# Two products in place of three per weight tile, for the 256-token stages of a two-layer diffusion backbone

## The chip, the cores and the metric

One core of a Trainium2 chip. The metric is the device time of one execution in microseconds, the median over runs. Compute engines of the core: TensorE (PE in the profile, with PEld for its weight loads), VectorE (DVE), ScalarE (ACT), GpSimd (POOL). SyncE (SP) issues the transfers. Matmuls write into PSUM, which the kernel uses as eight banks of 128 partitions x 512 fp32.

## The reference: what is computed

Two layers over 256 latent tokens with a prefix of 256 context tokens, width 1024. A layer is a half-step SwiGLU, a mixer and a second half-step SwiGLU, each behind an RMSNorm with shift, scale and gate:

```python
h = ffn_half_step(h, ...); hc = ffn_half_step(hc, ...)          # 1024 -> 2 x 2816 -> 1024
nq, nk, nv, fu, wq, wk, wv, gl = split_projection(u @ w_in[l])  # one combined projection
a = neighbourhood_attention(...); f = fourier_mix(fu); w = window_gqa_attention(...)
h = h + gt2 * merge_branches(a, f, w, gl, w_br[l], w_out[l])    # sigmoid gate per branch
if not last: (the same for the context tokens)
h = ffn_half_step(h, ...)
```

The context tokens are dropped after the mixer inputs of the last layer. So everything of layer 0, and of layer 1 up to the keys and values, runs over 512 tokens; the queries, gates, merge and second SwiGLU of layer 1 run over 256.

## The kernel before, in words

Activations lie transposed, 128 channels on the partitions and the tokens along the free dimension. To keep fp32 accuracy, each weight chunk and each activation is split into a high part (rounded to fp32r) and a low part (the rest). A product of a 128 x 128 weight tile with an activation is then three matmuls into one PSUM bank, `mm3` (lines 285 to 290): high weight with high activation (L288), high weight with low activation (L289), low weight with high activation (L290). For 512 tokens each of them has 512 columns, for 256 tokens 256.

Weights come in a fixed order as 424 chunks of eight tiles (`Weights`): a DMA on SP's queue, the high part on ACT (L66), the low part on DVE or POOL (L75, `lo_engine`), both some two chunks ahead of PE. `load_to`, `hi_to` and `lo_to` are called from `next`, so these instructions stand in the engines' queues where the weight stream crosses a chunk's start or middle. The program order is kept on each engine (`manual_schedule`); each engine works through its own queue in that order.

The stages of layer 1 that run over n = 256 tokens:

- `mix` (line 828 on; `attention` from line 694): `attention` goes step by step; a step issues, in this order, the normalising of older blocks (DVE L730 to L736), `small_part` (DVE L748), `transposes` (PE L741, ACT L743), `weights` of the block (DVE L717 takes the row maximum over the scores, then ACT L719 the exponentials), `values` (PE L759, ACT L765 at the end of a block), and then `fill`. `fill` first runs up to two pending pieces (`pieces`), then places projection matmuls among the steps. A pending piece is the taking out of a finished projection: `rope`, `plain`, or for gates `raw` (line 898 on: one ACT copy, L903, from PSUM to SBUF). Twelve of the 24 gate projections of layer 1 are placed in this way (`EARLY_GATES`); in attention the low weights are made on POOL.
- `merge` (line 1033 on): per output block j the remaining gate projections and their sigmoids (ACT L1052), three branch projections of four tiles, each multiplied with its gate on DVE (L1070), and the sum (L1073, L1074). The last block splits the seven earlier sums first (`split_s`), then its own. Then `project_out` with w_out.
- `ffn` (line 504 on) with n = 256: `first` makes four banks at once while the norm delivers its channels; then groups of 16 tiles, two banks each, taken out by `swish`: silu on ACT (L511), product on DVE (L512), high part on ACT (L297), low part on DVE (L298). Each half of 11 such groups is followed by `project_out` with w2, eight groups of 11 tiles, each taken out by `add_to_h` on DVE (L467).
- `stat` collects the squares for the next norm on POOL (last block: ACT L462), and the norm's chain (L173 to L191, L205 to L213) stands between `project_out` and the next stage; `finish` (L1084) writes the output.

Activations are tiles of 128 x 512 from one pool, `N_ACT` of them; the two parts of an activation are two tiles, also where only 256 of the 512 columns are used.

## Time and profile before

| | |
|---|---|
| median of 3 runs | 2100.93 us (2100.38 to 2104.16) |
| profiled execution, device time | 2101.61 us |
| its span in the trace | 2099.8 us |
| PE busy | 2049.5 us, 98% |
| DVE busy | 1282.1 us, 61% |
| ACT busy | 838.4 us, 40% |
| POOL busy | 340.6 us, 16% |

The 1.81 us between span and device time lie around the span. A busy PE is not PE at its peak: a matmul's record is longer than the step from one start to the next, so the steps have to be read from the order of time. Line numbers (L288) are those of the kernel before. In rows of the order of time the columns are the start, the time, the engine, the line and operation, the tiles, the count, and in brackets the idle time of the engine before it with what ended it.

### The profile page before, as it was taken

What the parts mean: (1) busy time and instruction counts of PE and PEld (TensorE: products, weight loads), DVE (VectorE), ACT (ScalarE), POOL (GpSimd) and SP (SyncE); (2) the same over time, 40 slices, a digit from 0 to 9 for tenths busy, and PEclk for the clock granted to TensorE, in tenths of its full rate; (3) what the DMA queues carried; (4) which work ended last, traced back from release to release, by engine and by line L of the source; (5) the groups of instructions that cost most, each with busy time, mean ns of one, the idle gap of its engine ahead of it and who ended that gap; (6) DMA issues with size and microseconds to landing.
All of it is one profiled execution on the core that took longest, in us unless ns stands there. A gap on an engine that the chain in (4) does not pass through costs nothing. (4 is left out here: it accounts for less than half of the span.)

```text
span 2099.8 us, 28967 instructions
## 1 busy us (share of the span) xinstructions
PE 2049.5 (98%) x11193; PEld 1764.6 (84%) x11193; DVE 1282.1 (61%) x2035; ACT 838.4 (40%) x1362; POOL 340.6 (16%) x238
## 2 busy tenths in 40 slices
PE   7999999999999999999999999999999989999998
PEld 2788888978888888988888898888888878999998
DVE  6777777465686335677777566533336568566554
ACT  4422222355787223432222243222224468645443
POOL 4200000402442111300000120000012155330002
PEclk8999999999999999999999999999999999999999
DMA  7455656445532333466666646623334463565653
GB/s 274 140 201 180 201 201 210 129 131 151 139 85 72 99 99 92 140 190 193 196 191 191 212 144 198 200 91 101 100 118 141 135 191 109 161 182 159 187 177 109
DMA packets 103010, 326.64 MB, mean 156 GB/s; under 512 B 13396, under 2 KB 18516, under 8 KB 102872
## 3 DMA queue, kind: packets, MB, share of 16 engines
q1 hardware_dynamic: 102872, 324.79, 49.6%
q8 instruction: 88, 1.44, 0.3%
q14 instruction: 50, 0.41, 0.1%
HBM read 305.60 MB, written 1.05 MB: 146 GB/s over the span
## 5 line engine op out<-in xcount | busy, mean ns | idle before, releaser
L289 PE MATMUL ps<-act,wh 128*128 128x512 f32 (+1 forms) x3227 | 1121.4, 348 | 10.6 <-DVE act L228 9.8
L288 PE MATMUL ps<-act,wh 128*128 128x512 f32 (+1 forms) x3227 | 1122.1, 348 | 2.1 <-ACT act L207 1.1
L290 PE MATMUL ps<-act,wl 128*128 128x512 f32 (+1 forms) x3227 | 1120.1, 347 | 1.8 <-DVE wl L75 1.8
L289 PEld LDWEIGHTS ps<-act,wh 128*128 128x128 f32 x3227 | 613.6, 190 | 86.7 <-DVE act L228 10.5
L290 PEld LDWEIGHTS ps<-act,wl 128*128 128x128 f32 x3227 | 613.7, 190 | 78.1 <-DVE wl L75 2.6
L288 PEld LDWEIGHTS ps<-act,wh 128*128 128x128 f32 x3227 | 613.6, 190 | 77.5 <-ACT act L207 1.4
L66 ACT ACTIVATE wh<-raw 128x1024 fp32r<-128x1024 f32 x424 | 436.4, 1050 | 318.4 <-PE ps L289 281.7
L75 DVE TENSOR_TENSOR wl<-raw,wh 128x1024 fp32r<-128x1024 f32 x379 | 473.3, 1261 | 102.6 <-ACT wh L66 102.6
L310 DVE CUSTOM_DVE_ANT_0 dump<-ada,silu_row 128x1024 bf16<-128x1024 f32 x224 | 273.4, 1221 | 12.2 <-DMA ada<-in_w_ada 9.9
L297 ACT ACTIVATE act<-tmp 128x512 fp32r<-128x512 f32 (+1 forms) x122 | 66.8, 566 | 431.5 <-DVE tmp L512 413.3
L450 POOL TENSOR_TENSOR tmp<-h 128x512 f32<-128x512 f32 (+1 forms) x7 | 11.4, 1634 | 1125.3 <-DVE h L467 797.6
L467 DVE SCALAR_TENSOR_TENSOR h<-ps,mod,h 128x256 f32<-128x256 f32 x136 | 61.7, 481 | 199.7 <-PE ps L290 199.7
L512 DVE TENSOR_TENSOR tmp<-tmp,ps 128x512 f32<-128x512 f32 (+1 forms) x88 | 54.6, 621 | 208.6 <-PE ps L290 203.1
L75 POOL TENSOR_TENSOR wl<-raw,wh 128x1024 fp32r<-128x1024 f32 x45 | 111.4, 2477 | 225.9 <-ACT wh L66 215.1
L298 DVE TENSOR_TENSOR act<-tmp,act 128x512 fp32r<-128x512 f32 (+1 forms) x122 | 74.3, 626 | 61.0 <-ACT act L297 61.0
L511 ACT ACTIVATE tmp<-ps 128x512 f32<-128x512 f32 (+1 forms) x88 | 47.8, 543 | 123.4 <-PE ps L290 122.8
L456 POOL TENSOR_TENSOR tmp<-h 128x256 f32<-128x256 f32 (+1 forms) x44 | 64.4, 1463 | 107.0 <-DVE h L467 104.4
L719 ACT ACTIVATE tmp<-tmp,sm 128x512 f32<-128x512 f32 (+1 forms) x96 | 62.1, 647 | 32.4 <-DVE sm L717 32.2
L748 DVE TENSOR_TENSOR act<-ps,act 128x512 fp32r<-128x512 f32 x80 | 54.9, 686 | 30.1 <-ACT act L743 27.5
L759 PE MATMUL ps<-act 128*128 128x256 f32 x320 | 62.5, 308 | 10.3 <-DVE act L748 9.2
L743 ACT ACTIVATE act<-ps 128x512 fp32r<-128x512 f32 x80 | 47.5, 594 | 46.2 <-PE ps L741 44.7
L1070 DVE TENSOR_TENSOR tmp<-tmp,ps 128x512 f32<-128x512 f32 (+1 forms) x48 | 26.0, 551 | 62.3 <-PE ps L290 61.0
(110 smaller groups left out, 1322.1 us busy)
## 6 DMA issues: line engine op xcount, KB each, us to landing
raw<-in_ws SPq DMA_DIRECT2D x424, 512.0 KB, 4.2
ada<-in_w_ada SPq DMA_DIRECT2D x128, 512.0 KB, 3.7
act<-act SPq DMA_DIRECT2D x112, 128.0 KB, 2.4
tmp<-in_w_ada_sc SPq DMA_DIRECT2D x16, 256.0 KB, 5.7
tmp<-in_w_ada SPq DMA_DIRECT2D x16, 256.0 KB, 6.0
masks<-in_na_bias SPq DMA_DIRECT2D x8, 512.0 KB, 5.0
h<-in_h SPq DMA_DIRECT2D x8, 256.0 KB, 5.5
act<-act SPq DMA_DIRECT2D x32, 64.0 KB, 3.4
```

The lines of the kernel that those rows point to most:

```text
L66: self.nc.scalar.activation(out=wh, in_=self.raw[i], func=AF.Copy)
L75: self.lo_engine.tensor_tensor(out=wl, in0=self.raw.pop(i), in1=self.hi[i].bitcast(F32), op=ALU.subtract)
L288: mm(ps, lhsT=w[0], rhs=x[0], start=start, stop=False)
L289: mm(ps, lhsT=w[0], rhs=x[1], start=False, stop=False)
L290: mm(ps, lhsT=w[1], rhs=x[0], start=False, stop=stop)
L297: nc.scalar.activation(out=hi, in_=src, func=AF.Copy)
L298: nc.vector.tensor_tensor(out=lo, in0=src, in1=hi.bitcast(F32), op=ALU.subtract)
L310: self.nc.vector.tensor_tensor_reduce(out=self.dump[:, ks], in0=w, in1=self.silu_row[:, v, ks], scale=1.0, scalar=m if half else 0.0, op0= ...
L456: nc.gpsimd.tensor_tensor(out=sq, in0=h, in1=h, op=ALU.mult)
L467: self.nc.vector.scalar_tensor_tensor(out=h, in0=ps, scalar=self.mod[l, g][:, v, j:j + 1], in1=h, op0=ALU.mult, op1=ALU.add)
L719: nc.scalar.activation(out=e[:, :nk], in_=e[:, :nk], func=AF.Exp, scale=-1.0, bias=nm, accum_out=b["sum"][:, i:i + 1])
L759: nc.tensor.matmul(b["ps"][hp][:, :256], lhsT=v, rhs=t[j][:, cs], start=c == 0 and j == 0, stop=c == n - 1 and j == 1)
```

## The change

For n = 256 the two parts of an activation now lie side by side in one 128 x 512 tile (`parts`, `pair`; the norm's output in a pool of its own, eight tiles [128, 2, 512], with `N_ACT` lowered from 60 to 44). `mm3` takes such a tile and makes two matmuls: the high weight with all 512 columns, which leaves high x high in the left half of the bank and high x low in the right half, and the low weight with the 256 high columns, added to the right half. Whoever takes the bank out adds the halves: `fold` copies the right half to SBUF on ACT and adds it to the left half, in PSUM, on DVE (in `swish` for both banks, in `merge` for each gate still to be made and each branch); `raw` has its ACT copy of the left half followed by a DVE addition of the right half; `project_out` calls `add_to_h` twice. It holds for the 12 early gates, for `merge`, w_out and the second SwiGLU of layer 1; with n = 512, and for the queries of layer 1, three products remain.

```diff
-N_ACT = 60
+N_ACT = 44
...
+        self.pair_p = pool("pair", KD)
...
+    def pair(self):
+        return self.pair_p.tile([128, 2, NT], F32R, tag="pair", name="pair")
+    def parts(self, n):
+        if n > NT // 2:
+            return self.act()[:, :n], self.act()[:, :n]
+        return self.act().rearrange("p (s t) -> p s t", s=2)
+    def fold(self, *pss):
+        n, t = NT // 2, self.tmp()
+        for i, ps in enumerate(pss):
+            self.nc.scalar.activation(out=t[:, i * n:i * n + n], in_=ps[:, n:], func=AF.Copy)
+        for i, ps in enumerate(pss):
+            self.nc.vector.tensor_tensor(out=ps[:, :n], in0=ps[:, :n], in1=t[:, i * n:i * n + n], op=ALU.add)
...
         mm = self.nc.tensor.matmul
+        if not isinstance(x, tuple):
+            half = lambda: mm(ps[:, NT // 2:], lhsT=w[1], rhs=x[:, 0, :], start=False, stop=False)
+            if stop:
+                half()
+            mm(ps, lhsT=w[0], rhs=x, start=start, stop=stop)
+            if not stop:
+                half()
+            return
...
+            if n < NT:
+                self.add_to_h(ps[:, :n], l, gate, j, 0)
+                self.add_to_h(ps[:, n:], l, gate, j, 0)
...
             s = self.tmp()
+            if n < NT:
+                self.fold(pa, pb)
             nc.scalar.activation(out=s[:, :n], in_=pa[:, :n], func=AF.Silu)
...
             nc.scalar.activation(out=t, in_=ps[:, :n], func=AF.Copy)
+            if n < NT:
+                nc.vector.tensor_tensor(out=t, in0=t, in1=ps[:, n:], op=ALU.add)
             res[name] = t
             yield
...
+                    if n < NT:
+                        self.fold(x)
                 nc.scalar.activation(out=t[:, :n], in_=x[:, :n], func=AF.Sigmoid)
...
-                    self.mm3(ps[:, :n], w, parts[b][k], k == 0, k == 3)
+                    self.mm3(ps, w, parts[b][k], k == 0, k == 3)
+                if n < NT:
+                    self.fold(ps)
                 nc.vector.tensor_tensor(out=sg[b][:, :n], in0=sg[b][:, :n], in1=ps[:, :n], op=ALU.mult)
```

## Rows read from the trace of the kernel before

**Rows 1.** The page, busy time of each engine over the span.

```profile
PE 2049.5 (98%) x11193; PEld 1764.6 (84%) x11193; DVE 1282.1 (61%) x2035; ACT 838.4 (40%) x1362; POOL 340.6 (16%) x238
```

**Rows 2.** Groups of instructions by line and shape, PE, whole span: one of the three products with 256 columns.

```profile
L288 PE MATMUL ps<-act,wh 128*128 128x256 f32 x1318 | 375.2, 285 | 2.1 <-ACT act L207 1.1 <-ACT act L297 0.8 <-ACT wh L66 0.2
```

**Rows 3.** Order of time on PE, a stretch of the second SwiGLU of layer 1 (256 columns): the first row and the 25th matmul after it.

```profile
1949.91 0.28 PE L290 MATMUL ps<-act,wl 128*128 128x256 f32 x1
...
1952.91 0.28 PE L288 MATMUL ps<-act,wh 128*128 128x256 f32 x1
```

**Rows 4.** The same for a stretch of layer 1 with 512 columns: the first row and the 8th matmul after it.

```profile
1349.62 0.39 PE L289 MATMUL ps<-act,wh 128*128 128x512 f32 x1
...
1351.43 0.39 PE L288 MATMUL ps<-act,wh 128*128 128x512 f32 x1
```

**Rows 5.** Busy time by stretch: us, PE, PEld, DVE, ACT, POOL (count each), granted clock of PE, DMA share, GB/s.

```profile
1700.00:1760.00 60.00, 50.52 (x379) 46.26 (x378) 44.23 (x92) 45.34 (x107) 34.14 (x27) 1.00 0.48 143
1760.00:1800.00 40.00, 39.71 (x316) 37.96 (x315) 24.92 (x53) 31.52 (x72) 19.33 (x10) 1.00 0.37 114
...
1900.00:2080.00 180.00, 180.00 (x1494) 180.00 (x1493) 102.27 (x129) 82.21 (x112) 10.40 (x8) 0.99 0.54 173
```

**Rows 6.** Busy time by stretch of 10 us, the same columns: two stretches in which PE stood idle.

```profile
1700.00:1710.00 10.00, 7.19 (x53) 6.24 (x52) 5.04 (x14) 6.03 (x13) 2.39 (x1) 1.00 0.61 246
...
1890.00:1900.00 10.00, 7.55 (x46) 6.67 (x45) 5.68 (x13) 4.67 (x8) 2.20 (x2) 0.78 0.29 95
```

**Rows 7.** The chain of work that ended last, pieces in order of time, within the attention of layer 1 (start, us, what).

```profile
1724.45 0.81 ACT tmp L719 x2
...
1749.89 0.27 ACT tmp L903
...
1774.53 0.62 PE ps L759 x3
```

**Rows 8.** Who waited for whom, same stretch (total us, times, longest): the second piece of `rope` on DVE behind its first on ACT.

```profile
DVE act L893 <- ACT act L891: 8.5, 5, 1.9
```

**Rows 9.** Order of time on ACT, attention of layer 1: gate copies (L903), and two of the exponentials (L719) behind the first and the third.

```profile
1726.75 0.39 ACT L903 ACTIVATE tmp<-ps 128x256 f32<-128x256 f32 x1
...
1727.51 0.72 ACT L719 ACTIVATE tmp<-tmp,sm 128x512 f32<-128x512 f32 x1
...
1736.43 0.37 ACT L903 ACTIVATE tmp<-ps 128x256 f32<-128x256 f32 x1
...
1749.79 0.36 ACT L903 ACTIVATE tmp<-ps 128x256 f32<-128x256 f32 x1
...
1750.54 0.72 ACT L719 ACTIVATE tmp<-tmp,sm 128x512 f32<-128x512 f32 x1
...
1766.40 0.38 ACT L903 ACTIVATE tmp<-ps 128x256 f32<-128x256 f32 x1
...
1771.00 0.36 ACT L903 ACTIVATE tmp<-ps 128x256 f32<-128x256 f32 x1
...
1778.38 0.39 ACT L903 ACTIVATE tmp<-ps 128x256 f32<-128x256 f32 x1
```

**Rows 10.** Order of time on DVE, same stretch: for each gate copy above the next long DVE instruction in program order, and for the first gate also the row maximum (L717) after it.

```profile
1724.41 0.67 DVE L748 TENSOR_TENSOR act<-ps,act 128x512 fp32r<-128x512 f32 x1
...
1726.06 0.69 DVE L717 CUSTOM_DVE_ANT_1 tmp<-ps,masks 128x512 f32<-128x512 f32 x1 [0.19 <-PE ps L708]
...
1735.68 0.69 DVE L748 TENSOR_TENSOR act<-ps,act 128x512 fp32r<-128x512 f32 x1 [0.30 <-ACT act L743]
...
1748.77 0.69 DVE L748 TENSOR_TENSOR act<-ps,act 128x512 fp32r<-128x512 f32 x1
1749.45 0.75 DVE L717 CUSTOM_DVE_ANT_1 tmp<-ps,masks,nsink 128x512 f32<-128x512 f32 x1
...
1764.06 0.69 DVE L748 TENSOR_TENSOR act<-ps,act 128x512 fp32r<-128x512 f32 x1 [1.01 <-ACT act L743]
...
1770.30 0.69 DVE L748 TENSOR_TENSOR act<-ps,act 128x512 fp32r<-128x512 f32 x1 [1.26 <-ACT act L743]
...
1776.04 0.69 DVE L748 TENSOR_TENSOR act<-ps,act 128x512 fp32r<-128x512 f32 x1 [0.82 <-ACT act L743]
```

**Rows 11.** Who waited for whom on PE (total us, times, longest), at the start of `merge` (1795 to 1812 us) and at its end (1860 to 1882 us).

```profile
PE ps L290 <- DVE wl L75: 0.8, 1, 0.8
```

```profile
PE ps L288 <- ACT act L297: 0.8, 1, 0.8
```

**Rows 12.** Order of time on DVE at the end of `merge`: two gate products in a row.

```profile
1867.92 0.74 DVE L1070 TENSOR_TENSOR tmp<-tmp,ps 128x256 f32<-128x256 f32 x2
```

**Rows 13.** Order of time on DVE, the taking out of one group of the second SwiGLU of layer 1, and on ACT the silu of the next.

```profile
1951.74 0.42 DVE L512 TENSOR_TENSOR tmp<-tmp,ps 128x256 f32<-128x256 f32 x1 [1.54 <-PE ps L290]
1952.64 0.42 DVE L298 TENSOR_TENSOR act<-tmp,act 128x256 fp32r<-128x256 f32 x1 [0.48 <-ACT act L297]
1953.59 2.36 DVE L75 TENSOR_TENSOR wl<-raw,wh 128x1024 fp32r<-128x1024 f32 x2 [0.53 <-ACT wh L66]
```

```profile
1954.55 0.38 ACT L511 ACTIVATE tmp<-ps 128x256 f32<-128x256 f32 x1
```

**Rows 14.** Order of time on DVE at the very end: the last `add_to_h`, and the eight multiplications of `finish`, of the same shape.

```profile
2089.91 0.48 DVE L467 SCALAR_TENSOR_TENSOR h<-ps,mod,h 128x256 f32<-128x256 f32 x1 [3.48 <-PE ps L290]
...
2093.16 3.22 DVE L1084 SCALAR_TENSOR_TENSOR tmp<-h,g_fin,ps 128x256 f32<-128x256 f32 x8 [1.04 <-PE ps L191]
```

More of the change, by code (lines that the diff above doesn't have):

```diff
@@ L202, in _step @@
             if v == 0:
-                self.u[k] = (em.act(), em.act())
+                self.u[k] = em.pair()
             hs = em.tmp()[:, :256]
@@ L206, in _step @@
                                            op0=ALU.mult, op1=ALU.mult)
-            nc.scalar.activation(out=self.u[k][0][:, s], in_=hs, func=AF.Identity, bias=sh[:, v, k:k + 1])
+            nc.scalar.activation(out=self.u[k][:, 0, s], in_=hs, func=AF.Identity, bias=sh[:, v, k:k + 1])
             self.work[t] = hs
@@ L211, in _step @@
             s = slice(v * 256, (v + 1) * 256)
-            hi, lo = self.u[k]
+            hi, lo = self.u[k][:, 0, :], self.u[k][:, 1, :]
             nc.vector.scalar_tensor_tensor(out=lo[:, s], in0=self.work.pop(t - 1), scalar=sh[:, v, k:k + 1],
@@ L221, in _first @@
         sh, sc = em.mod[self.l, 3 * self.g], em.mod[self.l, 3 * self.g + 1]
-        hi, lo = self.u[k] = em.act(), em.act()
+        self.u[k] = em.pair()
+        hi, lo = self.u[k][:, 0, :], self.u[k][:, 1, :]
         for out in (hi, u32):
@@ L277, in act, with two @@
         return self.act_p.tile([128, NT], F32R, tag="act", name="act")
+    def pair(self):
[4 more added lines that the diff above has]
+        return self.act().rearrange("p (s t) -> p s t", s=2)
+    def two(self, x):
+        return x if isinstance(x, tuple) else (x[:, 0, :], x[:, 1, :])
+    def fold(self, *pss):
[4 more added lines that the diff above has]
+            self.nc.vector.tensor_tensor(out=ps[:, :n], in0=ps[:, :n], in1=t[:, i * n:i * n + n], op=ALU.add)
     def tmp(self):
@@ L478, in group @@
                 w = self.W.next(tiles(j, k))
-                self.mm3(ps[:, :hi - lo], w, (x[k][0][:, lo:hi], x[k][1][:, lo:hi]), k == 0, k == kx - 1)
+                if n == NT:
+                    self.mm3(ps[:, :hi - lo], w, (x[k][0][:, lo:hi], x[k][1][:, lo:hi]), k == 0, k == kx - 1)
+                else:
+                    self.mm3(ps, w, x[k], k == 0, k == kx - 1)
+            if n < NT:
+                self.add_to_h(ps[:, :n], l, gate, j, 0)
+                self.add_to_h(ps[:, n:], l, gate, j, 0)
+                if nxt is not None:
+                    self.stat(j, 0, n)
+                return
             for v in range(lo // 256, hi // 256):
@@ L510, in swish @@
             s = self.tmp()
+            if n < NT:
+                self.fold(pa, pb)
             nc.scalar.activation(out=s[:, :n], in_=pa[:, :n], func=AF.Silu)
             nc.vector.tensor_tensor(out=s[:, :n], in0=s[:, :n], in1=pb[:, :n], op=ALU.mult)
-            gh, gl = self.act(), self.act()
-            self.split(s[:, :n], (gh[:, :n], gl[:, :n]))
-            return gh, gl
+            g = self.parts(n)
+            self.split(s[:, :n], self.two(g))
+            return g
         def first(passes):
@@ L534, in first @@
                             norm.stage2(1)
-                    x = tuple(t[:, lo:hi] for t in norm.u[k])
+                    x = norm.u[k][:, :, lo:hi]
+                    x = self.two(x) if n == NT else x
                     for q in range(4):
                         w = W.next((w13, l, k * 128, (q % 2) * DFF + (q // 2) * 128))
-                        self.mm3(pss[q][:, lo:hi], w, x, k == 0, k == KD - 1)
+                        self.mm3(pss[q][:, lo:hi] if n == NT else pss[q], w, x, k == 0, k == KD - 1)
             W.lo_engine = nc.vector
@@ L547, in ffn @@
                 u = norm.all()
-                ux = [(a[:, :n], b[:, :n]) for a, b in u]
+                ux = [self.two(a) if n == NT else a[:, :, :n] for a in u]
             self.W.on_tile = lambda: self.bg.step(1)
@@ L555, in ffn @@
                         w = W.next((w13, l, k * 128, ab * DFF + i * 128))
-                        self.mm3(pss[ab][:, :n], w, ux[k], k == 0, k == KD - 1)
+                        self.mm3(pss[ab], w, ux[k], k == 0, k == KD - 1)
                 g.append(swish(*pss))
@@ L581, in project_rows @@
                 s = slice(lo + t * 128, lo + (t + 1) * 128)
-                mm(ps, lhsT=u[k][0][:, s], rhs=w[0], start=k == 0, stop=False)
-                mm(ps, lhsT=u[k][0][:, s], rhs=w[1], start=False, stop=False)
-                mm(ps, lhsT=u[k][1][:, s], rhs=w[0], start=False, stop=k == KD - 1)
+                mm(ps, lhsT=u[k][:, 0, s], rhs=w[0], start=k == 0, stop=False)
+                mm(ps, lhsT=u[k][:, 0, s], rhs=w[1], start=False, stop=False)
+                mm(ps, lhsT=u[k][:, 1, s], rhs=w[0], start=False, stop=k == KD - 1)
         return pss
@@ L676, in along_channels @@
             ys[fc] = None
-            f = self.act()[:, :n], self.act()[:, :n]
+            f = self.parts(n)
             self.split(ps[:, :n].rearrange("p (s e k) -> p s e k", e=2, k=128),
-                       [a.rearrange("p (s k e) -> p s e k", e=2, k=128) for a in f])
+                       [a.rearrange("p (s k e) -> p s e k", e=2, k=128) for a in self.two(f)])
             out.append(f)
@@ L844, in project @@
             ps = self.ps()
+            side = name[0] == "gate" and n < NT
             for k in range(KD):
                 w = W.next(("w_in", l, k * 128, cols))
-                self.mm3(ps[:, :n], w, (u[k][0][:, :n], u[k][1][:, :n]), k == 0, k == KD - 1)
+                x = u[k][:, :, :n]
+                self.mm3(ps if side else ps[:, :n], w, x if side else self.two(x), k == 0, k == KD - 1)
                 if k == KD - 1:
@@ L984, in split_out @@
         def split_out(o, p):
-            hi, lo = self.act()[:, :n], self.act()[:, :n]
+            t = self.parts(n)
+            hi, lo = self.two(t)
             nc.scalar.activation(out=hi, in_=o[p][:, :n], func=AF.Copy)
@@ L989, in split_out @@
             nc.vector.tensor_tensor(out=lo, in0=o[p][:, :n], in1=hi.bitcast(F32), op=ALU.subtract)
-            o[p] = hi, lo
+            o[p] = t
         def left(o, p, lat):
@@ L1037, in split_s @@
         def split_s(x):
-            t = (self.act(), self.act())
-            self.split(x[:, :n], (t[0][:, :n], t[1][:, :n]))
-            return t[0][:, :n], t[1][:, :n]
+            t = self.parts(n)
+            self.split(x[:, :n], self.two(t))
+            return t
         def gates(j):
@@ L1050, in gates @@
                         w = W.next(("w_in", l, k * 128, O_GATE + b * D + j * 128))
-                        self.mm3(x[:, :n], w, (u[k][0][:, :n], u[k][1][:, :n]), k == 0, k == KD - 1)
+                        a = u[k][:, :, :n]
+                        self.mm3(x, w, a if n < NT else self.two(a), k == 0, k == KD - 1)
+                    if n < NT:
+                        self.fold(x)
                 nc.scalar.activation(out=t[:, :n], in_=x[:, :n], func=AF.Sigmoid)
```

## The prediction

> **What bounds the kernel now.** I read the page first: PE is busy 98% of the span, DVE 61%, ACT 40% [rows 1]. But a matmul's record is longer than its step, so the order of time on PE comes next, then the busy times by stretch. In the second SwiGLU of layer 1 the starts of 256-column matmuls follow each other without a gap: 25 steps in 3.00 us, 120.0 ns each [rows 3]; PE and its weight loads never pause from 1900 to 2080 us, while DVE works 102 of 180 us [rows 5]. That stretch is bound by PE's steps. The attention of layer 1 is another matter. From 1700 to 1760 us PE's records cover 50.5 of 60 us [rows 5], and the chain that ended last goes through exponentials on ACT and small parts on DVE until 1774 us, where PE takes over [rows 7]; one gate copy (L903) even lies on it. There the reader should see two in-order engines handing work back and forth, with PE waiting.
>
> **Fewer steps.** 880 weight tiles of layer 1 change: 352 of w13, 176 of w2, 192 of gates, 96 of branches, 64 of w_out. The count fits the row: 1318 matmuls of 256 columns on L288 [rows 2] are these, 64 for the queries (unchanged) and 374 that the 512-token stages make in halves. Now a tile costs 3 x 120.0 = 360.0 ns. A 512-column step is 1.81 us / 8 = 226.3 ns [rows 4], so the new tile costs 226.3 + 120.0 = 346.3 ns: the same 768 columns with one start less, 13.7 ns saved. I take both steps as they stand, although before no 512-column step alternates with a 256-column one and none reads its columns in two pieces (the norm's output does). Should the weight load behind the short step be what makes it 120.0, it would still be 120.0, for the load behind it is the same; a wider reach of the long step could bring it down to half of 226.3, a gain of 20.6 ns a tile, and with the two-piece read costing a tenth of a long step the saving would be gone. I take 13.7, since each step is read where PE does nothing else.
>
> Not all tiles pay: 96 belong to the early gates inside attention, about 19 stand right before PE's wait at the end of the merge, about 9 run at the lower clock after the norm. 756 x 13.7 ns = **-10.4 us**.
>
> A rule of the Trainium skill speaks against this term. The step at full clock exceeds its columns by 120.0 - 256/2.4 = 13.3 ns here [rows 3]. "TensorE: Matmul & The Clock Gate", in the section that asks why the gap is 56 ns and not 53.3 ns, gives a fixed cost of about 2.5 ns for each matmul; by it the 756 tiles would save 1.9 us, not 10.4. The trace does not agree with it: both widths here show some 13 ns.
>
> **The gates in attention.** `raw` was one ACT copy; now a DVE addition follows it at once. Order matters: the copy runs in `fill`, behind the exponentials of its own step (and at a block's end behind the four copies of `values`). DVE reaches the addition right after L717, and must stand there until ACT has done the exponentials and the copy. Behind it on DVE are the next step's normalising, its L748 (PE's `values` wait for it) and its L717 (the next exponentials wait for it). The trace has this very pattern already: the second piece of `rope` waits behind its first for 8.5 us in five times, 1.7 us each [rows 8]. Price for each gate: the copy's end, 0.05 for the signal, 0.37 for the addition (two like it take 0.74 [rows 12]), against the start of DVE's next L748 [rows 9, 10]:
> first gate 1727.14 + 0.42 = 1727.56 against 1724.41: 3.15;
> then 1737.22 - 1735.68 = 1.54; 1750.57 - 1748.77 = 1.80; 1767.20 - 1764.06 = 3.14; 1771.78 - 1770.30 = 1.48; 1779.19 - 1776.04 = 3.15. Together 14.3 us. The other six I put at nothing: they fall where DVE's next instruction starts about when the copy ends, or after the last exponentials, with PE the bound.
>
> Not all of it reaches the chain, since something waited anyway. Behind the first gate, L717 moves from 1726.06 to 1729.0, and the exponentials from 1727.51 to 1729.75: 2.2 of 3.15 us. Behind the third, L717 ends near 1751.95 and the exponentials move from 1750.54 to 1752.0: 1.45 of 1.80. That is 70 to 80%; 77% of 14.3 is **+11 us**. The last two fall where PE is about full [rows 5], so a late L748 is a PE stall there at once, and what was worked off is not given back: `fill` places the matmuls by step, not by time. Bounds: 4 us if the filler matmuls keep PE so busy that only every third stall shows, 15 if all of it does. I stay near the upper one, because the chain runs through just these instructions.
>
> **The merge.** At its start PE already waits 0.8 us for a low weight part [rows 11]; the change puts the copies and additions of the first branch banks ahead of it. One copy of about 0.38 and one addition of 0.37 is **+0.8 us** (0 to 2). At its end DVE works without a pause and PE waits 0.8 us for the last split [rows 11]; three additions of 0.37 more on DVE [rows 12] are **+1.1 us** (0 to 1.5). Between, DVE has room.
>
> **The ends.** `project_out` updates h twice. After w_out the norm's chain hangs on it, at the end of the kernel the output does; a second multiplication behind the first costs 3.22 / 8 = 0.40 us [rows 14]: **+0.8 us**. Longer waits could cost clock: after 2.8 us of idle in 10 us the granted clock stayed 1.00, and in the stretch around the norm it is 0.78 already [rows 6]; 0 to 1 us more, taken as 0.
>
> **The SwiGLU's own taking out.** A group lasts 16 x 346.3 ns = 5.54 us. Now DVE is through 4.2 us after the group's last matmul (product at 1951.74, two low weight parts done at 1955.95), with the silu of the first bank done during the second [rows 13]. With `fold`, the second bank's copy (0.43 with its signal) and silu or addition (0.4) come ahead of the product: 5.1 us, and the next first bank's addition of 0.37 makes 5.5. It just fits; the weights made two chunks ahead cover a late start. I take nothing; without that cover it costs what a cycle exceeds 5.54 us, twenty times. At the hand-over to w2, PE has ten tiles, 3.5 us, before it needs the last group, whose chain takes about 2.4.
>
> The pool changes (eight pair tiles against 16 single ones taken from `N_ACT`) leave as many tiles while a norm's output lives: nothing.
>
> **Sum.** -10.4 + 11 + 0.8 + 1.1 + 0.8 = +3.3 us. The profiled execution took 2101.6 (span 2099.8 and 1.8 around it), so 2104.9; the median of the runs lies 0.7 lower: **2104.2 us**.
>
> **Rivals.** (1) *Most of the gates' stalls are hidden.* PE has matmuls to run between steps, and DVE idles a quarter of that stretch [rows 5]. With 4 us in place of 11: -3.7 us, and a milder merge brings 2096.5 to 2097.5: about the bound of faster. Against it: the gate copy already on the chain [rows 7]. (2) *The SwiGLU's taking out becomes the bound.* From a cycle of 5.54 us on, each further 0.3 us costs 20 x 0.3 = 6 us: 2110, slower. For it: the 0.04 us that are left by the sum above. Against it: once DVE is late, ACT's copies lie ready and the cycle shrinks by their 0.4 us. (3) *The start saved is not saved*, as the steps alternate or the two-piece read is slow: 2104.2 + 10.4 = 2114.6. The fixed cost from the Trainium skill that is named above would put it at 2112.7.
>
> **How the numbers follow.** Forecast 0.62, its own range 2099 to 2108.5 by the gates' bounds; rival 1 0.21; rival 2 0.10; rival 3 0.04; 0.03 for what I have not seen. The measurement can tell about 0.2%, 4.2 us, from no change: faster is under 2096.7, slower over 2105.1. Of the forecast's chance 0.43 lies within, 0.19 above; rival 1 gives 0.17 to faster and 0.04 to the same; rivals 2 and 3 are slower. So 0.17, 0.47, 0.36. The range runs from 2096.5 to 2110.5.
>
> **What would show it.** Right: in the second SwiGLU of layer 1 PE's starts alternate 226 and 120 ns and that stretch is some 7 us shorter; in attention DVE's waits on L903 appear, 1.5 to 3 us each, and it is some 11 us longer; PE's waits at the merge grow by about 1 us each. Wrong: no DVE wait behind L903, or an attention that is no longer than before (then faster); a tile that costs 360 ns as now; or PE waiting for low weight parts every group in the SwiGLU.

## The result and the profile after

After the change the kernel takes 2122.31 us (median of 4 runs, 2119.69 to 2123.61) against 2102.55 us (4 runs, 2100.38 to 2106.21): ratio 1.0091, 95% interval 1.0071 to 1.0110: 19 us slower, clear of the noise. The forecast was 2104.2 us with a range up to 2110.5, so the time lies 11.8 us above the range. The profiled execution has a span of 2121.4 us, 21.6 more than that of before; the medians lie 2.5 us closer together than these two executions.

Five landmarks, read from the order of time of both kernels, show where the time went (start, us, line numbers of before and after; the net column is the growth within each stage):

| landmark | before | after | later by | net |
|---|---|---|---|---|
| last early gate copied (L903, L949) | 1797.3 | 1815.9 | 18.6 | +18.6 |
| last gate product of the merge (L1070, L1124) | 1869.7 | 1891.3 | 21.6 | +3.0 |
| first norm update after w_out (L205) | 1895.92 | 1919.62 | 23.7 | +2.1 |
| last silu (L511, L554) | 2055.35 | 2079.68 | 24.3 | +0.6 |
| end of the span | 2099.8 | 2121.4 | 21.6 | -2.7 |

So the attention of layer 1 is 18.6 us longer, the merge with w_out 5.1, and from the norm to the end only 2.1 us are won back. The last silu is a lagging landmark: a group is taken out later than before, so the last two rows belong together.

The page of after, busy time of PE (compare [rows 1]): 880 matmuls fewer and still nearly the same busy time. Records overlap and waits came in besides, so this row alone tells nothing.

```profile
PE 2048.4 (97%) x10313; PEld 1721.3 (81%) x10313; DVE 1327.4 (63%) x2151; ACT 863.8 (41%) x1442; POOL 338.7 (16%) x238
```

**Attention.** Who waited for whom in after, 1700 to 1820 us (total us, times, longest):

```profile
DVE tmp L951 <- ACT tmp L949: 27.1, 12, 3.9
...
PE ps L803 <- DVE act L792: 20.1, 12, 2.8
ACT tmp L763 <- DVE sm L761: 17.4, 14, 4.3
```

The same view of before, 1700 to 1802 us (L759, L748, L719 and L717 there are L803, L792, L763 and L761 here):

```profile
DVE act L748 <- ACT act L743: 11.9, 13, 1.8
ACT tmp L719 <- DVE sm L717: 9.4, 11, 1.6
...
PE ps L759 <- DVE act L748: 6.9, 6, 2.2
```

The first row is new: DVE stands 27.1 us at the twelve additions of `raw`, waiting for ACT's copy. The rows under it are the price: PE's wait for `values` grows from 6.9 to 20.1 us, that of the exponentials from 9.4 to 17.4. The wait L748 <- L743 of before shrinks to 1.7 us in after (3 times): 10.2 us of DVE's standing only took its place. 27.1 us of waits and 12 x 0.37 = 4.4 us of additions, less 10.2, make about 21; 18.6 show at the end of the stage.

Order of time on DVE in after: the twelve additions, the wait before each in brackets.

```profile
1726.87 0.42 DVE L951 TENSOR_TENSOR tmp<-tmp,ps 128x256 f32<-128x256 f32 x1 [2.74 <-ACT tmp L949]
1740.81 0.42 DVE L951 TENSOR_TENSOR tmp<-tmp,ps 128x256 f32<-128x256 f32 x1 [1.46 <-ACT tmp L949]
1757.22 0.42 DVE L951 TENSOR_TENSOR tmp<-tmp,ps 128x256 f32<-128x256 f32 x1 [1.52 <-ACT tmp L949]
1767.81 0.42 DVE L951 TENSOR_TENSOR tmp<-tmp,ps 128x256 f32<-128x256 f32 x1 [1.34 <-ACT tmp L949]
1776.11 0.42 DVE L951 TENSOR_TENSOR tmp<-tmp,ps 128x256 f32<-128x256 f32 x1 [3.88 <-ACT tmp L949]
1783.42 0.42 DVE L951 TENSOR_TENSOR tmp<-tmp,ps 128x256 f32<-128x256 f32 x1 [1.88 <-ACT tmp L949]
1791.41 0.42 DVE L951 TENSOR_TENSOR tmp<-tmp,ps 128x256 f32<-128x256 f32 x1 [3.55 <-ACT tmp L949]
1796.99 0.42 DVE L951 TENSOR_TENSOR tmp<-tmp,ps 128x256 f32<-128x256 f32 x1 [2.22 <-ACT tmp L949]
1805.20 0.42 DVE L951 TENSOR_TENSOR tmp<-tmp,ps 128x256 f32<-128x256 f32 x1 [2.48 <-ACT tmp L949]
1809.68 0.42 DVE L951 TENSOR_TENSOR tmp<-tmp,ps 128x256 f32<-128x256 f32 x1 [2.86 <-ACT tmp L949]
1815.23 0.42 DVE L951 TENSOR_TENSOR tmp<-tmp,ps 128x256 f32<-128x256 f32 x1 [2.84 <-ACT tmp L949]
1816.31 0.42 DVE L951 TENSOR_TENSOR tmp<-tmp,ps 128x256 f32<-128x256 f32 x1 [0.33 <-ACT tmp L949]
```

In program order the prediction had priced the first, second, third, fifth, sixth and seventh; here these wait 15.0 us together. The fourth, the eighth and the last four, put at nothing, wait 12.1 us.

Where the stage grows can be read from the starts of ACT's twelve gate copies (us, from the order of time on ACT):

| gate | 1 | 2 | 3 | 4 | 5 | 6 | 7 | 8 | 9 | 10 | 11 | 12 |
|---|---|---|---|---|---|---|---|---|---|---|---|---|
| before | 1726.75 | 1736.43 | 1749.79 | 1758.25 | 1766.40 | 1771.00 | 1778.38 | 1781.77 | 1787.24 | 1790.56 | 1796.13 | 1797.32 |
| after | 1726.45 | 1740.41 | 1756.81 | 1767.42 | 1775.70 | 1783.02 | 1791.00 | 1796.59 | 1804.78 | 1809.27 | 1814.82 | 1815.90 |
| later by | -0.3 | 4.0 | 7.0 | 9.2 | 9.3 | 12.0 | 12.6 | 14.8 | 17.5 | 18.7 | 18.7 | 18.6 |

Between a priced gate's copy and the next copy the stage grows by 4.3, 3.0, 2.2, 2.7, 0.6 and 2.2 us, 15.0 together. Behind the fourth, eighth and ninth it grows by 0.1, 2.7 and 1.2 us, 4.0 together, and behind the tenth and eleventh by nothing. To give each growth to the gate ahead of it is a reading by place; no run took gates out one by one.

The chain that ended last shows what such a wait does (after, the ninth gate, which has no exponential ahead of it; start, us, what): four copies of `values` on ACT (the last is shown), the gate copy, the addition, the small part, and only then PE's `values`.

```profile
1804.38 0.38 ACT tmp L809
1804.78 0.39 ACT tmp L949
1805.20 0.42 DVE tmp L951
1805.62 0.61 DVE act L792
1806.28 0.62 PE ps L803 x3
```

Before, PE worked through this part of the attention without a gap (39.71 of 40 us up to 1800 [rows 5]). In after the cover is gone: PE's records fill 5.92 of the 10 us up to 1800. The granted clock, 1.00 in every stretch of 10 us of this stage in before, falls in some stretches, to 0.83 in the first row. Busy times by stretch (columns as in [rows 5]):

```profile
1730.00:1740.00 10.00, 7.62 (x43) 6.71 (x42) 6.30 (x13) 5.74 (x12) 3.85 (x3) 0.83 0.36 97
...
1790.00:1800.00 10.00, 5.92 (x40) 5.16 (x39) 6.29 (x14) 6.05 (x13) 4.70 (x4) 1.00 0.24 61
```

**The merge.** PE's waits in after, at its start (1816 to 1832 us, two rows) and at its end (1878 to 1900 us, two rows), where [rows 11] had one of 0.8 us each (and before another of 0.2 at the start):

```profile
PE ps L313 <- DVE wl L75: 1.8, 1, 1.8
PE ps L316 <- ACT wh L66: 0.3, 1, 0.3
...
PE ps L313 <- ACT act L329: 2.3, 1, 2.3
PE ps L313 <- DVE wl L75: 1.9, 1, 1.9
```

Order of time on DVE at that end: the splits, then low part, addition (L300) and product (L1124) in turn without a pause. The last split ends at 1893.5, and w_out can't go on before it.

```profile
1884.11 2.97 DVE L330 TENSOR_TENSOR act<-tmp,act 128x256 fp32r<-128x256 f32 x7
1887.00 1.21 DVE L75 TENSOR_TENSOR wl<-raw,wh 128x1024 fp32r<-128x1024 f32 x1
1888.13 0.42 DVE L300 TENSOR_TENSOR ps<-ps,tmp 128x256 f32<-128x256 f32 x1
1888.59 0.42 DVE L1124 TENSOR_TENSOR tmp<-tmp,ps 128x256 f32<-128x256 f32 x1
...
1893.07 0.42 DVE L330 TENSOR_TENSOR act<-tmp,act 128x256 fp32r<-128x256 f32 x1 [0.54 <-ACT act L329]
```

**The SwiGLU.** Order of time on ACT in after, the silu of two groups that lie four apart:

```profile
1952.76 0.38 ACT L554 ACTIVATE tmp<-ps 128x256 f32<-128x256 f32 x1
...
1975.32 0.38 ACT L554 ACTIVATE tmp<-ps 128x256 f32<-128x256 f32 x1
```

22.56 us / 4 = 5.64 us for 16 tiles: 352.5 ns a tile, where it was 360.0 ([rows 3], three steps) and 346.3 was forecast. PE's starts don't alternate 226 and 120 ns: from 2018 to 2074 us the wide step takes 235.6 and the narrow one 117.0 in the mean. Order of time on PE in w2, where the wide step reads 512 columns that lie in one piece, the same place (two narrow products in a row) in two banks of 11 tiles that lie seven apart: 27.17 us / 77 = 352.9 ns a tile.

```profile
2082.60 0.40 PE L313 MATMUL ps<-act,wl 128*128 128x256 f32 x2
...
2109.77 0.40 PE L313 MATMUL ps<-act,wl 128*128 128x256 f32 x2
```

DVE takes a group out as forecast and still has time left at the end of the cycle (order of time on DVE, compare [rows 13]); PE has no wait for a low part in that stretch.

```profile
1958.53 0.43 DVE L300 TENSOR_TENSOR ps<-ps,tmp 128x256 f32<-128x256 f32 x1 [0.55 <-ACT tmp L298]
1959.07 0.42 DVE L555 TENSOR_TENSOR tmp<-tmp,ps 128x256 f32<-128x256 f32 x1
1959.97 0.42 DVE L330 TENSOR_TENSOR act<-tmp,act 128x256 fp32r<-128x256 f32 x1 [0.48 <-ACT act L329]
1960.92 2.36 DVE L75 TENSOR_TENSOR wl<-raw,wh 128x1024 fp32r<-128x1024 f32 x2 [0.53 <-ACT wh L66]
1963.20 0.42 DVE L300 TENSOR_TENSOR ps<-ps,tmp 128x256 f32<-128x256 f32 x1
```

### The profile page after: what moved, and what is told of

Read it like the earlier page. It is cut to its first block, busy times and chain, and to the rows that moved or that the text cites. A ratio compares the mean times of both kernels' runs of the same rounds, so it can differ in the third digit from the quotient of the medians.

```text
span 2121.4 us, 27459 instructions
## 1 busy us (share of the span) xinstructions
PE 2048.4 (97%) x10313; PEld 1721.3 (81%) x10313; DVE 1327.4 (63%) x2151; ACT 863.8 (41%) x1442; POOL 338.7 (16%) x238
## 5 line engine op out<-in xcount | busy, mean ns | idle before, releaser
L321 PE MATMUL ps<-pair,wh 128*128 128x512 f32 (+1 forms) x1536 | 581.5, 379 | 13.3 <-DVE pair L229 12.5
L320 PE MATMUL ps<-pair,wh 128*128 128x512 f32 (+1 forms) x1536 | 581.5, 379 | 0.0
L322 PE MATMUL ps<-pair,wl 128*128 128x512 f32 (+1 forms) x1536 | 580.4, 378 | 1.0 <-DVE wl L75 0.9
L321 PEld LDWEIGHTS ps<-pair,wh 128*128 128x128 f32 x1536 | 291.0, 189 | 66.7 <-DVE pair L229 13.6
L322 PEld LDWEIGHTS ps<-pair,wl 128*128 128x128 f32 x1536 | 290.9, 189 | 54.4 <-DVE wl L75 1.4
L320 PEld LDWEIGHTS ps<-pair,wh 128*128 128x128 f32 x1536 | 290.8, 189 | 52.3 <-ACT tmp L227 0.9
L320 PE MATMUL ps<-act,wh 128*128 128x512 f32 (+1 forms) x811 | 290.2, 358 | 0.1
L321 PE MATMUL ps<-act,wh 128*128 128x512 f32 (+1 forms) x811 | 289.6, 357 | 0.2 <-DVE act L330 0.2
L322 PE MATMUL ps<-act,wl 128*128 128x512 f32 (+1 forms) x811 | 289.5, 357 | 0.0
L342 DVE CUSTOM_DVE_ANT_0 dump<-ada,silu_row 128x1024 bf16<-128x1024 f32 x224 | 273.3, 1220 | 12.7 <-DMA ada<-in_w_ada 10.4
L316 PE MATMUL ps<-pair,wh 128*128 128x512 f32 x544 | 193.4, 404 | 1.7 <-DVE pair L213 1.7
L321 PEld LDWEIGHTS ps<-act,wh 128*128 128x128 f32 x811 | 153.3, 189 | 22.7 <-DVE act L330 0.5
L320 PEld LDWEIGHTS ps<-act,wh 128*128 128x128 f32 x811 | 153.3, 189 | 22.6 <-ACT act L329 0.5
L322 PEld LDWEIGHTS ps<-act,wl 128*128 128x128 f32 x811 | 153.3, 189 | 22.0
L313 PE MATMUL ps<-pair,wl 128*128 128x256 f32 x544 | 144.2, 285 | 0.8 <-DVE wl L75 0.8
```

What stands on the lines that cost most here:

```text
L313: half = lambda: mm(ps[:, NT // 2:], lhsT=w[1], rhs=x[:, 0, :], start=False, stop=False)
L316: mm(ps, lhsT=w[0], rhs=x, start=start, stop=stop)
L320: mm(ps, lhsT=w[0], rhs=x[0], start=start, stop=False)
L321: mm(ps, lhsT=w[0], rhs=x[1], start=False, stop=False)
L322: mm(ps, lhsT=w[1], rhs=x[0], start=False, stop=stop)
L342: self.nc.vector.tensor_tensor_reduce(out=self.dump[:, ks], in0=w, in1=self.silu_row[:, v, ks], scale=1.0, scalar=m if half else 0.0, op0= ...
```

## Experiments

The theory: the early gates' additions hold DVE in the attention (most of the loss), the merge loses at its ends, and the tiles save less than forecast. The rivals: the products themselves or the new layout cost, or the merge pays in every column. Ratios are to before, which ran beside each group of experiments, with 95% intervals of 0.1 to 0.2% to either side, 2 to 4 us. Differences between experiments go by these ratios. In an edit `...` stands for lines not shown; where one thing is undone in several places, one is shown.

**1. The early gates alone undone.** Three products and the copy alone.

```diff
-            side = name[0] == "gate" and n < NT
+            side = False
...
-            if n < NT:
-                nc.vector.tensor_tensor(out=t, in0=t, in1=ps[:, n:], op=ALU.add)
```

> The changed kernel, with the 12 early gates back to three products and to the one ACT copy; merge, w_out and SwiGLU stay side by side. Theory S (VectorE stands behind the gate copies in attention): the stretch from 1700 us to the last early gate copy goes from 116 us back to some 97, and the kernel from 2122 to 2103.5 (2101 to 2106). Rival W (the attention is longer for another reason: smaller pool of tiles, pairs as operands, the lower clock): the stretch stays above 112 us, the kernel above 2117.

Measured: 2107.34 us, 1.0016 (1.0007 to 1.0025). The last gate copy starts at 1799.5 instead of 1815.9, and PE's wait for `values` is what it was in before (1700 to 1820 us). The time lies 1.3 us above the 2101 to 2106 of theory S, far under rival W's 2117:

```profile
PE ps L803 <- DVE act L792: 6.9, 7, 2.1
```

1.0091 - 1.0016 = 0.75%, 15.8 us (give or take 4.5): the early gates are most of the loss. The merge, still side by side, takes 76.9 us from there to the last gate product, against 72.4 in before.

**2. The addition one fill later.** All products as in the change; DVE reaches the addition when the copy is over.

```diff
             if n < NT:
+                yield 1
                 nc.vector.tensor_tensor(out=t, in0=t, in1=ps[:, n:], op=ALU.add)
```

> The changed kernel, with the addition of an early gate put off to the next step's fill, one step after its ACT copy. Same instructions, another place in VectorE's queue. Theory S: no wait of VectorE on the gate copy is left and the kernel takes 2104 (2101 to 2108). Rival D (it is the work of the twelve additions on a full VectorE, 12 x 0.37 us, and what follows from it, not the standing): no more than 3 us come back, 2119 or more.

Measured: 2111.05 us, 1.0035 (1.0021 to 1.0048), between the two theories and 3 us above the range of theory S; last copy at 1802.1. The wait at the addition is all but gone:

```profile
DVE tmp L952 <- ACT tmp L949: 0.7, 2, 0.5
```

With the same products and the same twelve additions the stage is 13.8 us shorter than in the change, and the kernel 0.56%, 11.8 us. So the place is most of the price. The 0.19%, 4.0 us (give or take 3.4), that lie between this run and experiment 1 stay with the products and additions at their later place.

**3. The wait alone, put into the kernel before.** Its products and its layout are untouched; an addition whose result nothing reads follows each of the twelve copies.

```diff
             nc.scalar.activation(out=t, in_=ps[:, :n], func=AF.Copy)
+            if n < NT:
+                nc.vector.tensor_tensor(out=self.tmp()[:, :n], in0=t, in1=ps[:, :n], op=ALU.add)
             res[name] = t
```

> The kernel before, with three products everywhere, and only this added: behind the ACT copy of each of the 12 early gates of layer 1 an addition on VectorE that reads the copy and the bank and writes a tile that nobody reads. Theory S: attention grows by 15 to 19 us as in the changed kernel, 2118 to 2121. Rival W: 2103 to 2107.

Measured: 2120.36 us, 1.0082 (1.0065 to 1.0098); last copy at 1816.1, 18.8 us late, as in the change. Who waited for whom, 1700 to 1820 us:

```profile
DVE tmp L905 <- ACT tmp L903: 27.9, 12, 3.6
...
PE ps L759 <- DVE act L748: 19.5, 13, 3.1
```

One instruction placed right behind another engine's, twelve times, makes the loss of the attention without the products, the layout and the pools of the change. (It also takes a tile and holds its bank a little longer, which was not tried apart.)

**4. The layout alone.** Pair tiles and pools of the change, three products everywhere, no additions.

```diff
...
-                        self.mm3(pss[ab], w, ux[k], k == 0, k == KD - 1)
+                        self.mm3(pss[ab][:, :n], w, self.two(ux[k]), k == 0, k == KD - 1)
...
```

> The layout of the change alone: parts side by side, pool of pairs, 44 tiles, but three products, one update of h and no folding anywhere. Theory S: within 2 us of the kernel before, 2100.5 to 2104.5. Rival W: the tiles or their pool cost part of the 20 us, 2108 or more.

Measured: 2103.47 us, 1.0003 (0.9994 to 1.0012): nothing that can be told, as the prediction had it.

**5. Fewer changes of width.** The whole change, with the narrow products of four tiles put together.

```diff
-            mm(ps, lhsT=w[0], rhs=x, start=start, stop=stop)
-            if not stop:
-                half()
+            if not stop:
+                mm(ps, lhsT=w[0], rhs=x, start=start, stop=False)
+            self.halves.append(half)
+            if stop or len(self.halves) == 4:
+                for half in self.halves:
+                    half()
+                self.halves = []
+            if stop:
+                mm(ps, lhsT=w[0], rhs=x, start=start, stop=stop)
```

> The changed kernel, with the two widths in runs instead of in turn: four 512-column products, then their four 256-column ones (at a bank's end the last wide one comes last, as in the change). Same instructions, another order on TensorE. Theory A (a change of width costs time, so that a tile takes 352.5 ns where the two steps by themselves make 346.3): a group of 16 tiles in the second SwiGLU goes from 5.64 us to 5.57, the kernel from 2122 to 2118.5 (2116 to 2120). Rival L (the long step is longer for its own sake, as two pieces or as the one that covers two halves of the bank): the group stays at 5.64 us, the kernel at 2121 to 2124.

Measured: 2123.16 us, 1.0096 (1.0082 to 1.0110). In the SwiGLU the groups come every 5.59 us instead of 5.64, as looked for, but the whole is no shorter, a miss: last copy to last gate product takes 76.3 us (75.4 in the change), and PE's wait for the split at the merge's end is 3.1 us (2.3).

**6. Only SwiGLU and w_out side by side.** Early gates and merge with three products.

```diff
...
-                        self.mm3(x, w, a if n < NT else self.two(a), k == 0, k == KD - 1)
-                    if n < NT:
-                        self.fold(x)
+                        self.mm3(x[:, :n], w, self.two(a), k == 0, k == KD - 1)
...
```

> The changed kernel with three products for the early gates and in the whole merge (late gates and branches, no folding there); w_out and the second SwiGLU stay side by side. Theory M (the merge loses by the copies and additions on ScalarE and VectorE, 4.5 us over its 72, more than its 192 tiles save): merge from the last early gate copy to the last gate product back from 76.9 to 72.4 us, the wait for the last split back to 1 us, kernel 2102 (2100 to 2104), 4 to 6 us under the one with the gates alone put back. Rival F (the merge breaks even, what is lost is lost in the SwiGLU and the norms): 2106 to 2108.

Measured: 2100.36 us, 0.9990 (0.9981 to 0.9999). The merge is back at 72.4 us. Against experiment 1 that is 0.26%: the merge side by side costs 5.5 us (give or take 2.7). From the last copy to the first norm update, w_out included, it is 98.85 us here and 105.03 in experiment 1.

**7 and 8. The same with runs of four and of eight.** Edit as in 5, for experiment 8 with 8 in place of 4.

> The same as the kernel with gates and merge in three products, and the widths in runs of four in what is left side by side (w_out and SwiGLU, 592 tiles). Theory A: another 592 x 4.4 ns = 2.6 us less, 2099.5 (2097.5 to 2101.5), below the kernel before. Rival L: no difference to it.

> As the kernel with gates and merge in three products and runs of four in w_out and SwiGLU, but runs of eight: one change of width and back per bank of eight tiles in place of two. Theory A (what a tile takes above 346.3 ns belongs to the changes of width): the group of 16 tiles, 5.64 us in turn and 5.59 in runs of four, goes to 5.56; the kernel is within 1.5 us of the one with runs of four, 2098 to 2100.5. Rival L (a rest of 3 ns a tile belongs to the wide step itself): the group stays at 5.59.

Measured: 2099.60 us, 0.9975 (0.9966 to 0.9984), and 2098.27 us, 0.9972 (0.9962 to 0.9983). Order of time on ACT with runs of eight, the silu of the first and the last of eleven groups:

```profile
1998.17 0.38 ACT L559 ACTIVATE tmp<-ps 128x256 f32<-128x256 f32 x1
...
2054.04 0.38 ACT L559 ACTIVATE tmp<-ps 128x256 f32<-128x256 f32 x1
```

55.87 / 10 = 5.587 us, 349.2 ns a tile; runs of four give 5.594 us, 349.6. So the group did not go to the 5.56 of theory A: 2.9 ns a tile are left above 346.3, as rival L had it. In a bank of eight tiles the width changes 14 times in turn, 4 times in runs of four, twice in runs of eight.

The rest is nevertheless not the wide step's own. Order of time on PE with runs of eight, one run of eight wide products (the last of a bank and seven of the next), the last three of the same run, the eight narrow ones, and the next wide one:

```profile
2011.43 0.40 PE L323 MATMUL ps<-pair,wh 128*128 128x512 f32 x1
...
2012.59 0.84 PE L316 MATMUL ps<-pair,wh 128*128 128x512 f32 x3
2013.27 1.11 PE L314 MATMUL ps<-pair,wl 128*128 128x256 f32 x8
2014.22 0.40 PE L323 MATMUL ps<-pair,wh 128*128 128x512 f32 x1
```

The last three wide steps take (2013.27 - 2012.59) / 3 = 227 ns, like the 226.3 of [rows 4], though they too read two pieces and cover both halves of the bank. The first five take (2012.59 - 2011.43) / 5 = 232 ns. The narrow ones take 0.95 us / 8 = 119 ns. So in w13 the excess lies in the wide steps that follow a change of width, and lasts for some five of them. In w2, whose wide runs have nine products and two, no wide step settles at 227 in this run. Why a wide step is longer behind narrow ones is not shown.

**9 and 10. SwiGLU alone side by side**, w_out with three products too: in turn, and in runs of four.

```diff
...
-                if n == NT:
+                if n == NT or gate == 5:
...
```

> The change in the second SwiGLU of layer 1 alone (528 tiles in turn, 352.5 ns each): gates, merge and w_out with three products. What is saved is 528 x 7.5 ns = 4.0 us, less 0.4 for the second update of h at the end and about 1 for the foldings behind the norm: 2100.5 to 2101, 2 to 3 us under the kernel before. Against the kernel that has w_out side by side too (64 tiles, 0.5 us saved, 0.4 and a later last split lost): no difference that can be told.

> The SwiGLU alone, with runs of four: 528 tiles at 349.3 ns save 5.6 us, less the same 1.4: 2099 to 2100, the fastest of these. If the runs of four cost at the banks' ends what they save between, it is as the one in turn, 2101.

Measured: 2100.59 us, 0.9988 (0.9979 to 0.9997), and 2098.78 us, 0.9977 (0.9968 to 0.9986). w_out side by side is worth nothing that can be told. The SwiGLU in turn is worth 0.15% against experiment 4, 3.2 us (give or take 2.7).

**11 and 12. Which columns of the merge cost time.** On the kernel of experiment 1, the last column with three products; and on that of experiment 8, only the columns 1 to 6 side by side (`range(1, 7)`).

```diff
...
-                    self.mm3(ps, w, parts[b][k], k == 0, k == 3)
-                if n < NT:
+                    if n < NT and j in range(0, 7):
+                        self.mm3(ps, w, parts[b][k], k == 0, k == 3)
+                    else:
+                        self.mm3(ps[:, :n], w, self.two(parts[b][k]), k == 0, k == 3)
+                if n < NT and j in range(0, 7):
                     self.fold(ps)
```

> The early gates with three products, SwiGLU and w_out side by side in turn, and the merge side by side in its first seven columns; the last column has three products and no addition. Theory A (the merge loses at its two ends, where the added copies and additions stand before splits and low parts that TensorE needs next): at the end of the merge TensorE's waits go back from 2.3 + 1.9 us to about 0.9, the start keeps its 1.8; time 2107.3 - 3.3 = 2104, last gate copy to last gate product about 75 us. Theory B (every column of the merge pays, since VectorE and ScalarE get more to do throughout): 7/8 of the 5.5 us between the kernel with the merge in three (2100.4) and the one with it side by side (2107.3) by ratios stay, 2106.5, and the waits at the end stay above 2 us.

> SwiGLU and w_out side by side with runs of eight; the early gates with three products; the merge side by side only in its columns 1 to 6. Theory A (the merge loses at its ends alone): waits of TensorE at both ends as before (0.8 and 0.9 us), and some 120 tiles of the merge gain about 10 ns each: 1.2 us less than with the merge in three (2098.3), so 2097, and last gate copy to last gate product 71.2 us against 72.4. Theory B (every column pays): 6/8 of 5.5 us more, 2102.4, and 75 us or more between those two.

Measured for the first: 2101.92 us, 0.9994 (0.9985 to 1.0002). One column of eight undone gives back 0.22%, 4.6 of the 5.5 us (give or take 2.7), more than theory A asked for. From the last copy to the last gate product it is 74.8 us, as theory A had it, and to the first norm update 101.05, so 4.0 of the 6.2 us that experiment 6 gave back. PE's waits at the end (1860 to 1882 us) are 1.9 us together, where theory A had 0.9:

```profile
PE ps L313 <- DVE wl L75: 1.0, 1, 1.0
PE ps L313 <- ACT act L329: 0.9, 1, 0.9
```

Measured for the second: 2097.72 us, 0.9970 (0.9960 to 0.9980), the lowest ratio here, though not to be told from experiment 8. The middle columns cost nothing that can be told, so theory B fails. They gain nothing either. Last copy to last gate product is 71.5 us, under the 72.4 of three products, but last copy to first norm update is 99.6 us, against 98.4 in experiment 8. At the end PE waits 2.1 us for the last split, where theory A had 0.9 and experiment 8 has 1.1. DVE needs 7.5 us from the start of the seven splits to the last split in both runs, without a pause up to the last sum; PE comes there 1 us sooner and waits 1 us longer. In the 5 us from 1870 on the granted clock is 0.67, where experiment 8 has 1.00.

## Why the prediction was wrong

By parts, with the ratios of the experiments (the first difference good to 4.5 us, the others to some 2 or 3; the parts add up to the whole by the way they are formed):

| part | predicted us | measured us | from |
|---|---|---|---|
| early gates | +11.0 | +15.8 | change less 1 |
| merge (173 tiles less its waits) | -2.4 + 1.9 = -0.5 | +5.5 | 1 less 6 |
| w_out (64 tiles, one h update) | -0.9 + 0.4 = -0.5 | +0.4 | 6 less 9 |
| SwiGLU (519 tiles, one h update) | -7.1 + 0.4 = -6.7 | -3.2 | 9 less 4 |
| layout and pools | 0 | +0.6 | 4 |
| sum | +3.3 | +19.1 | |

The direction of both large parts, gates and SwiGLU, was right, that of the merge was not. Three steps failed: the price of the early gates, the ends of the merge, and the saving of a tile.

**The price of the early gates.** The stall itself was the right mechanism, and its size at the six gates that were priced was right: 14.3 us is how much later DVE's next L748 was to start, and four of these L748 had waits of their own in before, 3.4 us together [rows 10], so 17.7 us of standing and adding were forecast; 15.0 + 6 x 0.37 = 17.2 are found. Two steps behind that failed.

The first is the share that reaches the chain: "77% of 14.3 is +11 us". The stage grows by 15.0 us behind these six gates (13.9 in experiment 3, read the same way), more than the whole of the 14.3, so whatever was absorbed, as much came in besides. The first gate shows how: L717 was forecast at 1729.0 and starts at 1730.88, because the pair of scalings ahead of it takes 3.0 us instead of 0.88 (last section). Behind it the granted clock falls as well, to 0.83 from 1730 to 1740 us.

The second is the zero: "The other six I put at nothing: they fall where DVE's next instruction starts about when the copy ends, or after the last exponentials, with PE the bound." They wait 12.1 us, and the stage grows by 4.0 us behind three of them (3.7 in experiment 3), nearly all of it behind the eighth and ninth. Their places were read from the trace of before. Once the first gates have pushed the stage apart, PE no longer has work in hand at 1790 to 1800 us, the eighth and ninth gate stand on the chain, and the copies of `values` are as long a queue ahead of a gate copy as exponentials are. From the tenth gate on the chain does run on PE's filler matmuls, so there the cover held: waits of 2.86 and 2.84 us leave the last copy where it was. The two steps are worth about 4 us each; the bound of "15 if all of it does" was used up by the six priced gates alone.

Experiment 3 shows that the wait with its addition makes the 18.6 us of the stage, experiment 2 that the additions at a later place cost some 3 to 5 us (1802.1 against 1799.5 in experiment 1 and 1797.3 in before).

How the 18.6 us divide among standing, clock and slower normalising stays open. The clock can be bounded: 0.83, 0.83, 0.92 and 0.91 in four stretches of 10 us make 10 x 2 x (0.17 + 0.17 + 0.08 + 0.09) = 10.2 us at 1.2 GHz, half of which, 5.1 us, would be lost if PE were the bound all that time. Before had 1.00 throughout, experiment 3 has 10.2 us by the same sum, and experiment 2 has 6.8 us with a stage only 4.8 us longer. The scalings can be bounded as well (last section): they take 3.7 us more than in before, in experiment 3 only 1.3. "0 to 1 us more, taken as 0", said for the norm, was not asked for the attention at all.

**The ends of the merge.** "+0.8 us" and "+1.1 us" counted the added instructions one by one, and took the savings of the tiles in between as gains. PE's waits there went from 1.8 to 6.3 us. Experiment 11 shows that the last column makes most of the loss: 4.6 of 5.5 us by ratio, 4.0 of 6.2 by the landmarks. DVE had no pause there already, from 1863.9 us to the last sum; each addition also needs ACT's copy first, so the products come later, and the low parts of w_out, queued behind them on DVE, come late as a second wait (1.9 us) that the prediction did not have. The middle of the merge costs nothing that can be told, as forecast, but what its tiles save doesn't reach the norm (experiment 12), so the 2.4 us counted for the merge's tiles were not there to be had.

**13.7 ns a tile.** "I take both steps as they stand, although before no 512-column step alternates with a 256-column one and none reads its columns in two pieces." A tile saves 7.5 ns. The missing 6.2 go with the change of width from step to step, or with the order of the weight loads that changes along with it: runs of four give back 2.9 and runs of eight 3.3 of them, and with runs of eight the wide steps of w13 are down to 227 ns, the size taken, after five of a kind (experiments 7 and 8). The two-piece read and the two halves of the bank are cleared by the same steps, and w2, which reads in one piece, takes 352.9 ns in turn, w13 in two pieces 352.5. At 7.5 ns the 756 tiles are worth 5.7 us, not 10.4. So rival 3 came true by half.

The Trainium skill, "TensorE: Matmul & The Clock Gate", section "Wait — 56ns, not 53.3ns?", gives a fixed 2.5 ns for each matmul; by it, as an estimate, a tile would save 2.5 ns. The trace gives 7.5 in turn and 10.8 in runs of eight, so the figure does not carry over to these products, each of which loads its own weights; in turn the truth lies about midway between it and the forecast.

**What held.** Rival 1 fell: the stalls were not hidden. Rival 2 fell: the SwiGLU's taking out fits the cycle. The second h update is 0.52 us (the pair takes 1.00, one 0.48 [rows 14]) against 0.40 forecast. Layout and pools cost nothing that can be told. The chance of slower was put at 0.36, under that of the same, and the largest term of the sum had a price for half of its instructions only.

## What to carry to other kernels

An instruction placed on an in-order engine right behind one of another engine's queue costs that queue's length, not its own: 0.37 us became 2.3 us in the mean, and the work behind it moved. Price every place where it stands, all of them, as if the ones before had already pushed the stage apart: "PE is the bound there" is true of the old trace only. Saving work is worth something where the engine is the bound and its helpers have room up to the end of the stretch (the SwiGLU, 0.15% in turn); at the seams the same edit lengthens the chain, and what is saved just ahead of a seam is spent waiting there (the middle columns). So do it by stretch and leave the seams as they were (experiment 12, with runs of eight: ratio 0.9970 against 1.0091).

## What the runs showed of the hardware

Steps of two widths cost more in turn than apart: 352.5 ns for 512 and 256 columns in turn, 349.2 ns with eight of a kind together, where 226.3 and 120.0 add up to 346.3. In w13 with runs of eight, the first five wide steps behind narrow ones take 232 ns in the mean and the last three 227.

The normalising on DVE (L780, two scalings) takes 0.88 us by itself and 2.70 us where POOL makes a low part of the weights at that moment. Order of time in after, DVE (two rows), then POOL:

```profile
1792.61 0.88 DVE L780 TENSOR_SCALAR tmp<-tmp,sm 128x512 f32<-128x512 f32 x2
...
1799.43 2.70 DVE L780 TENSOR_SCALAR tmp<-tmp,sm 128x512 f32<-128x512 f32 x2
```

```profile
1799.05 2.40 POOL L75 TENSOR_TENSOR wl<-raw,wh 128x1024 fp32r<-128x1024 f32 x1 [0.34 <-ACT wh L66]
```

Of the ten pairs of scalings from 1724 us to the end of the stage the longest takes 3.61 us in the change and 3.27 in experiment 3 (each beside a low part and another instruction of POOL), but 1.89 in before, 1.90 in experiment 1 and 1.84 in experiment 2. The ten take 9.5 us more than 0.88 each in the change, 5.8 in before, 7.1 in experiment 3 and 5.6 in experiment 1. That the stalls of DVE move ACT's weight copies, and so POOL's low parts, onto the scalings is a reading and not shown: experiment 2 has a pair of 3.29 us at 1717.8 us, ahead of its first gate copy. What this adds to the 18.6 us was not tried by itself; from before it is 3.7 us in the change and 1.3 in experiment 3, so most of the loss stands without it. The Trainium skill, "SBUF — State Buffer", section "Who interferes with whom", says that a `tensor_scalar` in a two-port mode and a GpSimd instruction exclude each other for the whole of an instruction; the rows agree, 0.88 us alone and 2.70 beside 2.40 us of POOL; which mode these scalings run in, no run here shows.
